# An encoder trunk in split float32 on one core: both heads' products ahead of their squares, low parts last in attention, and one transpose a tick sooner

## The chip, the cores and the metric

The kernel runs on one core of a Trainium2 chip. The metric is the device time of one execution in microseconds; a time that is quoted for a kernel is the median of several executions. One further execution is taken by the hardware profiler; all rows of a profile and a trace are from that one.

## The reference

The reference is an encoder trunk of two layers over 256 tokens of width 1024, all in float32. Cut to what the change touches, one layer is:

```python
u = rms_norm(h, g_mix_pre)
(gq, gk, gv, gg, ra_f, ra_b, aq, ak, av, gate_a, gate_b) = jnp.split(u @ w_in, offsets, axis=-1)
# branch A: gated linear attention in both directions, 4 heads, 128 keys and 256 values each
o_gla    = rms_norm(o_f + o_b, g_gla_out)            # one root per token and head
branch_a = (o_gla * silu(gg)) @ w_o_gla
# branch B: softmax attention, 8 query heads of 128, 2 key heads, all 256 tokens are keys
branch_b = gqa_attention(q, k, v) @ w_o_attn
# merge, then the output projection
mixed = sigmoid(gate_a) * branch_a + sigmoid(gate_b) * branch_b
h = h + rms_norm(mixed @ w_out, g_mix_post)
# then a SwiGLU feed-forward block and an input embedding, each added to h
```

## The kernel before, in words

**Products in three matmuls.** Each float32 operand is split into a high part, a cast to TensorE's reduced format by ScalarE (ACT), and a low part, the difference, by VectorE (DVE). Both stand in `split` (line 133). A product is then three matmuls: high by high, and each high by the other's low. `mm3` (lines 107 to 111, its matmuls carry line 105) does the three of one part one after another. `passes` (line 113, its matmuls carry line 121) takes several parts of one sum: first two matmuls of every part, then the third of every part. Without `fresh` the first two are high by high and low by high, and the last one reads the low part of the second operand. With `fresh` the low part of the first operand comes last.

**Tiles and order.** Tokens stand in two halves of 128. All PSUM tiles (`acc`, `aux`) are 128x512, one of eight banks each. Weights are streamed by DMA into `raw` or `lent` tiles, cast and subtracted into `wh` and `wl`, and used from there. Side work is written as generators that are resumed by ticks: a matmul loop over weights (`amode`) gives ticks, two for 12 matmuls of 512 columns, and `yield n` lets n ticks pass. The tables `W` and `WAIT_...` hold these numbers, and with a list of priorities they set the order in which each engine's program is written; every engine runs its own program in that order.

**GLA outputs.** `outputs(hf, pr)` (from line 1309) is called four times per layer, for each half and pair of heads. Two heads share one PSUM bank `o`, 256 columns each. For each head come six matmuls and, in the kernel before, directly behind them a Square on ACT (line 1324) that sums the squares of its 256 columns into `ss`. GpSimd (POOL) makes the inverse root (lines 465 and 466), and VectorE scales both heads out of PSUM into `on` (line 517). When all are done, `out_gate` takes the sigmoid of the output gate on ACT (line 1388), multiplies on VectorE (line 126), and PE transposes the result (line 447, tile `aux_0gg`).

**Attention.** `attend` (from line 1187) computes, for one key head and one half of the queries, the softmax, transposes the probabilities for both halves of the keys (`turn_p`, line 1176), splits them into `pT` (tiles `mid_..at`), and multiplies them with the values (`avh`, `avl`) into `aux_..at`: two parts, six matmuls of 512 columns. There are eight such products, four a layer.

**The merge.** `merge` multiplies both branches with their sigmoids; when the second is added (line 1451), a task `turn` is queued that waits `WAIT_MIX[hf]` ticks and then transposes four 128x128 blocks into `mixT` (`transpose_in`, line 447, split by line 133). The output projection (`by_half`, line 719; matmuls `acc_..wout`) reads `mixT`, half 0 first, in two parts `kh` of four blocks each. It starts with the first part of half 0.

Of the kernel before, what the change touches and what calls it, by code (L numbers as in the profile page):

```python
# [13 lines left out]
AF = mybir.ActivationFunctionType  # L14
# [3 lines left out]
P = 128  # L18
# [8 lines left out]
WAIT, WAIT_FIRST, WAIT_FFN, WAIT_BLOCK = 6, 4, 4, 6  # L27

WAIT_NEXT, WAIT_IN, WAIT_H = (7, 11), ((6, 9), (6, 6)), ((3, 5), (3, 5))
WAIT_MIX = 4, 6  # L30
WAIT_SPREAD = 12
W = dict(r=5, z=6, s0=4, s=3, s1=9, o0=1, o=1, k=4, q=3, a0=1, a1=4, a2=4, a3=1, g=6)

# [26 lines left out]
def trunk_kernel(ctx: ExitStack, tc: tile.TileContext, a: dict, out: bass.AP):  # L60
# [25 lines left out]
    def big(dt=F32):  # L86
        return bigp.tile([P, 2048], dt, tag="big", name=nm("big"))

    def mid(dt=F32):
        return b4p.tile([P, 1024], dt, tag="mid", name=nm("mid"))  # L90

    def acc():
        return accp.tile([P, 512], F32, tag="acc", name=nm("acc"))

    def aux():
        return accp.tile([P, 512], F32, tag="acc", name=nm("aux"))
# [4 lines left out]
    def small(n, tag, bufs=None):  # L101
        return smp.tile([P, n], F32, tag=tag, name=nm(tag), **({"bufs": bufs} if bufs else {}))

    def mm(o, lhsT, rhs, start, stop):
        return nc.tensor.matmul(o, lhsT, rhs, start=start, stop=stop)  # L105

    def mm3(o, l, r, start, stop):
        (lh, ll), (rh, rl) = l, r
        mm(o, lh, rh, start, False)
        mm(o, lh, rl, False, False)  # L110
        mm(o, ll, rh, False, stop)

    def passes(o, parts, start, stop, fresh=False, between=None, **kw):

        ps = [((xh, yh), (xh, yl), (xl, yh)) if fresh else ((xh, yh), (xl, yh), (xh, yl)) for (xh, xl), (yh, yl) in parts]
        seq = [p for t in ps for p in t[:2]] + [t[2] for t in ps]
        for n, (x, y) in enumerate(seq):  # L120
            nc.tensor.matmul(o, x, y, start=start and n == 0, stop=stop and n == len(seq) - 1, **kw)  # L121
            if between is not None and 2 * (n + 1) == len(seq):
                between()
# [7 lines left out]
    def split(hi, lo, src):  # L131

        return nc.scalar.copy(hi, src), nc.vector.tensor_tensor(out=lo, in0=src, in1=hi.bitcast(F32), op=ALU.subtract)  # L133
# [325 lines left out]
    def inv_sqrt(t, n, mul, add, eps=None):  # L459

        with in_turn():
            if eps is None:
                nc.gpsimd.tensor_scalar(out=t, in0=t, scalar1=mul, scalar2=add, op0=ALU.mult, op1=ALU.add)
            else:
                nc.gpsimd.tensor_scalar(out=t, in0=t, scalar1=eps, scalar2=mul, op0=ALU.add, op1=ALU.mult)
        last_pow[0] = nc.gpsimd.tensor_tensor(out=t, in0=t, in1=neghalf[:, :n], op=ALU.pow)
# [49 lines left out]
    def scale_gain(out, in0, r, g):  # L516
        nc.vector.scalar_tensor_tensor(out=out, in0=in0, scalar=r, in1=g, op0=ALU.mult, op1=ALU.mult)

    def halves(t):
        return [t[:, j * 512 : (j + 1) * 512] for j in range(2)]  # L520
# [180 lines left out]
    def project_t(sp):  # L701

        o = [acc(), acc()]
        for kh in range(2):
            wmode(o, sp, kh * 4, ws.take(), kh == 0, kh == 1)
            ws.done()
        return o

    def project(sp):

        o = [acc(), acc()]
        for kh in range(2):
            w = ws.take()
            for hf in range(2):
                amode(o[hf], sp, hf, kh * 4, w, kh == 0, kh == 1)
            ws.done()
        return o
# [81 lines left out]
    ss = [small(2, "ss") for _ in range(2)]  # L799
# [176 lines left out]
    for l in range(DEPTH):  # L976
# [108 lines left out]
        o = {}  # L1085
# [18 lines left out]
        kTh, kTl, avh, avl = (kv4[:, i * 512 : (i + 1) * 512] for i in range(4))  # L1104
# [71 lines left out]
        def turn_p(pr_):  # L1176
            res = []
            for s in range(2):
                ps = aux()
                for i in range(4):  # L1180
                    nc.tensor.transpose(ps[:, i * P : (i + 1) * P], pr_[:, i, s * P : (s + 1) * P], ident)
                pT = halves(mid(F32R))
                split(pT[0], pT[1], ps)
                res.append(pT)
            return res

        def attend(g):
            qs = []
            for hf in range(2):
                yield W["q"]  # L1190
                ps = aux()
                for i in range(4):
                    hd = 4 * g + i
                    nc.tensor.transpose(ps[:, i * P : (i + 1) * P], qrs[hf][:, hd * P : (hd + 1) * P], ident)
                qh, ql = halves(mid(F32R))
                split(qh, ql, ps)
                qs.append((qh, ql, qss[hf][:, 4 * g : 4 * g + 4]))
            keys.need()
            yield W["a0"]
            prs = []  # L1200
            for hf in range(2):
                prs.append(softmax(g, hf, qs[hf]))
                yield W["a1"]
            for hf in range(2):
                pT = turn_p(prs[hf])
                yield W["a2"]
                o = aux()
                for s in range(2):
                    vs = slice(s * 256 + g * P, s * 256 + (g + 1) * P)
                    mm3(o, (avh[:, vs], avl[:, vs]), pT[s], s == 0, s == 1)  # L1210
                aT.put(o, 4 * g, 4, hf * P, P)
                yield W["a3"]

        def attention():
            for g_ in range(2):
                part[0] = f"{l}at{g_}"
                yield from attend(g_)
# [9 lines left out]
        for x in range(2):  # L1227
            o = project_t(uT)
# [81 lines left out]
        on = big().rearrange("p (s c) -> p s c", s=2)  # L1310

        def outputs(hf, pr):

            o = aux()
            ss = small(8, "hss")
            for i in range(2):
                hd = 2 * pr + i
                c = slice(hd * 256, (hd + 1) * 256)
                oh = o[:, i * 256 : (i + 1) * 256]
                for s in range(2):  # L1320

                    idx = hf if s == hf else (2 if s == 0 else 3)
                    mm3(oh, [t[:, hd, idx, :] for t in sc], [t[:, s, c] for t in v], s == 0, s == 1)
                nc.scalar.activation(
                    on[:, hf, c], oh, AF.Square, scale=1.0 / 16.0, accum_out=ss[:, i : i + 1]
                )
            inv_sqrt(ss[:, 0:2], 2, 1.0, EPS, eps_out[hf])
            for i in range(2):
                hd = 2 * pr + i
                scale_gain(  # L1330
                    on[:, hf, hd * 256 : (hd + 1) * 256], o[:, i * 256 : (i + 1) * 256], ss[:, i : i + 1], ggla
                )
# [39 lines left out]
        for j in range(2):  # L1372
            o = project(uT)
# [72 lines left out]
        def merge(br):  # L1446
            def then(j, hf, o):
                sl = [s[:, hf, j * 512 : (j + 1) * 512] for s in sgate[: br + 1]]
                vmul(sl[br], o, sl[br])
                if br == 1:  # L1450
                    nc.vector.tensor_tensor(out=sl[0], in0=sl[0], in1=sl[1], op=ALU.add)

                    def turn():
                        yield WAIT_MIX[hf]
                        transpose_in(mixT, sl[0], 4 * j, 4, hf)
# [57 lines left out]
        for hf in range(2):  # L1513
            ws.lend = hf == 1
            for b in range(2):
                o = acc()
# [51 lines left out]
        o = []  # L1568
# [138 lines left out]
```

## Time and profile before

| | |
|---|---|
| time, median of 3 runs | 920.82 us (920.67 to 921.23) |
| profiled execution | 920.53 us, of which the span is 918.8 us |
| granted TensorE clock | 0.998 |
| TensorE (PE) busy | 909.9 us, 4673 matmuls |
| PE's weight loads (PEld) | 776.1 us |
| VectorE (DVE) | 785.2 us |
| ScalarE (ACT) | 583.1 us |
| GpSimd (POOL) | 93.1 us |
| moved by DMA | 173.44 MB, 188 GB/s over the span |

In the rows that follow, a row of the timeline has the start in us from the span's start, the busy time of the group, the engine, the line of the kernel, the operation, what it writes and reads (tile names with their numbers left out, the layer is the digit in the name), the shape, and how many instructions the row holds. Behind it, in brackets, stands the idle time ahead of it and what ended that. Ends of matmuls are modelled; their starts are not. The waits view has for each pair of waiting and releasing tile the time, how often, and the longest. The view of stretches has a stretch's length, the busy time and the number of instructions of PE in it, the granted clock, the DMA share and GB/s.

### The profile page before, as it was taken

To read this page: it belongs to the slowest core of one execution; us is meant where nothing else is said; L and a number is where in the kernel's file an instruction comes from. 1 tells how busy PE (TensorE), PEld (TensorE's weight loads), DVE (VectorE), ACT (ScalarE), POOL (GpSimd) and SP (SyncE) were. 2 spreads that over 40 slices of the span, in tenths; PEclk is the share of its full clock that TensorE was granted. 3 is DMA by queue.
4 is the path that set the end of the run, shared out by engine and by line. 5 is a ranking of instruction groups with operands and counts; after the bars stand their busy time and mean duration, and the time that the engine had idled before them with its cause. 6 is when DMAs were issued, how large, how long until landed. Compare 5 with 4: busy or idle time off the path is not lost.

```text
span 918.8 us, 12423 instructions
## 1 busy us (share of the span) xinstructions
PE 909.9 (99%) x4673; PEld 776.1 (84%) x4673; DVE 785.2 (85%) x1004; ACT 583.1 (63%) x968; POOL 93.1 (10%) x149
## 2 busy tenths in 40 slices
PE   9999999999999999999999999999999999999996
PEld 8998888888888888888899988888888888888886
DVE  6988989987669998999779789798875799989984
ACT  6688767564567565567675677765644766565563
POOL 3700212310000000000114001100001000000000
PEclk9999999999999999999999999999999999999999
DMA  8664445657385655657576424454673856555361
GB/s 277 206 199 135 138 138 189 212 184 244 107 298 183 210 197 189 244 158 260 195 238 210 158 92 138 138 202 164 201 256 103 278 170 212 215 173 225 124 243 46
DMA packets 88679, 173.44 MB, mean 189 GB/s; under 512 B 3422, under 2 KB 26470, under 8 KB 88108
## 3 DMA queue, kind: packets, MB, share of 16 engines
q1 hardware_dynamic: 88316, 172.27, 55.1%
q8 instruction: 36, 0.59, 0.3%
q10 hardware_dynamic: 304, 0.40, 0.1%
q14 instruction: 23, 0.19, 0.1%
HBM read 169.50 MB, written 3.15 MB: 188 GB/s over the span
## 4 chain that ended last, share of the span: by engine, by line
PE 92%; DVE 4%; issue 1%; ACT 1%; POOL 1%; DMA 1%; POOLq 0%; DVEq 0%; SPq 0%; ACTq 0%
PE acc_1ffnin L121 11%; PE acc_0ffnin L121 11%; PE acc_0gate L121 7%; PE acc_1gate L121 7%; PE acc_1ffnin L105 7%; PE acc_0ffnin L105 6%; PE acc_1rq L121 3%; PE acc_0gqk L121 3%; PE acc_0wout L121 2%; PE acc_1gqk L121 2%; PE acc_0ple L121 2%; PE acc_1gg L121 2%; PE acc_0v L121 2%; PE acc_0merge L121 2%; PE acc_1merge L121 2%; PE acc_1ple L121 2%
## 5 line engine op out<-in xcount | busy, mean ns | idle before, releaser
L105 PE MATMUL acc_0ffnin<-wh_0ffnin,big_0ffnin 128*128 128x512 f32 x176 | 57.0, 393 | 0.1
L105 PE MATMUL acc_1ffnin<-wh_1ffnin,big_1ffnin 128*128 128x512 f32 x176 | 56.8, 392 | 0.0
L133 ACT CAST wh_1ffnin<-raw_1ffnin 128x1024 fp32r<-128x1024 f32 x38 | 38.5, 1049 | 27.1 <-DMA raw_1ffnin<-in_w_ffn_out_dram 8.6
L133 ACT CAST wh_0ffnin<-raw_0ffnin 128x1024 fp32r<-128x1024 f32 x38 | 38.2, 1048 | 24.9 <-PE acc_0ffnin L121 7.4
L133 DVE TENSOR_TENSOR wl_1ffnin<-raw_1ffnin,wh_1ffnin 128x1024 fp32r<-128x1024 f32 x38 | 45.0, 1223 | 8.8 <-ACT wh_1ffnin L133 8.7
L133 DVE TENSOR_TENSOR wl_0ffnin<-raw_0ffnin,wh_0ffnin 128x1024 fp32r<-128x1024 f32 x38 | 44.7, 1222 | 8.1 <-ACT wh_0ffnin L133 8.0
L121 PE MATMUL acc_0ffnin<-wh_0ffnin,big_0wout 128*128 128x512 f32 x168 | 42.5, 393 | 0.0
L121 PE MATMUL acc_1ffnin<-wh_1ffnin,big_1wout 128*128 128x512 f32 x168 | 42.5, 393 | 0.0
L105 PEld LDWEIGHTS acc_0ffnin<-wh_0ffnin,big_0ffnin 128*128 128x128 f32 x176 | 33.0, 188 | 7.2 <-DVE big_0ffnin L133 0.5
L105 PEld LDWEIGHTS acc_1ffnin<-wh_1ffnin,big_1ffnin 128*128 128x128 f32 x176 | 33.0, 188 | 6.7
L133 DVE TENSOR_TENSOR wl_1ffnin<-lent_1ffnin,wh_1ffnin 128x1024 fp32r<-128x1024 f32 x30 | 35.9, 1221 | 1.7 <-ACT wh_1ffnin L133 1.7
L133 DVE TENSOR_TENSOR wl_0ffnin<-lent_0ffnin,wh_0ffnin 128x1024 fp32r<-128x1024 f32 x30 | 35.9, 1221 | 1.7 <-ACT wh_0ffnin L133 1.7
L121 PEld LDWEIGHTS acc_1ffnin<-wh_1ffnin,big_1wout 128*128 128x128 f32 x168 | 31.1, 188 | 6.2
L121 PEld LDWEIGHTS acc_0ffnin<-wh_0ffnin,big_0wout 128*128 128x128 f32 x168 | 31.1, 188 | 6.2
L133 ACT CAST wh_1ffnin<-lent_1ffnin 128x1024 fp32r<-128x1024 f32 x30 | 30.7, 1052 | 7.3 <-PE acc_1ffnin L105 3.9
L133 ACT CAST wh_0ffnin<-lent_0ffnin 128x1024 fp32r<-128x1024 f32 x30 | 30.7, 1054 | 7.0 <-PE acc_0ffnin L105 3.9
L105 PE MATMUL acc_1ffnin<-wl_1ffnin,big_1ffnin 128*128 128x512 f32 x88 | 34.3, 390 | 0.0
L105 PE MATMUL acc_0ffnin<-wl_0ffnin,big_0ffnin 128*128 128x512 f32 x88 | 34.3, 390 | 0.0
L133 DVE TENSOR_TENSOR wl_0gate<-raw_0gate,wh_0gate 128x1024 fp32r<-128x1024 f32 x20 | 24.3, 1260 | 5.3 <-ACT wh_0gate L133 5.2
L133 ACT CAST wh_0gate<-raw_0gate 128x1024 fp32r<-128x1024 f32 x20 | 20.0, 1049 | 13.1 <-DMA raw_0gate<-in_w_o_attn_dram 6.3
L133 DVE TENSOR_TENSOR wl_1gate<-raw_1gate,wh_1gate 128x1024 fp32r<-128x1024 f32 x20 | 23.6, 1223 | 5.4 <-ACT wh_1gate L133 5.2
L133 ACT CAST wh_1gate<-raw_1gate 128x1024 fp32r<-128x1024 f32 x20 | 20.0, 1049 | 11.7 <-DMA raw_1gate<-in_w_o_attn_dram 5.7
(710 smaller groups left out, 2705.4 us busy)
## 6 DMA issues: line engine op xcount, KB each, us to landing
raw_0ffnin<-in_w_ffn_out_dram SPq DMA_DIRECT2D x11, 1024.0 KB, 5.6
raw_1ffnin<-in_w_ffn_out_dram SPq DMA_DIRECT2D x11, 1024.0 KB, 5.2
lent_0ffnin<-in_w_ffn_in_dram SPq DMA_DIRECT2D x6, 1024.0 KB, 7.7
lent_1ffnin<-in_w_ffn_in_dram SPq DMA_DIRECT2D x6, 1024.0 KB, 6.7
raw_0v<-in_w_in_dram SPq DMA_DIRECT2D x4, 1024.0 KB, 4.9
raw_0gate<-in_w_o_gla_dram SPq DMA_DIRECT2D x4, 1024.0 KB, 5.2
raw_0gate<-in_w_o_attn_dram SPq DMA_DIRECT2D x4, 1024.0 KB, 5.6
raw_0wout<-in_w_ffn_in_dram SPq DMA_DIRECT2D x8, 512.0 KB, 5.0
```

The costliest lines, as they stand in the source:

```text
L105: return nc.tensor.matmul(o, lhsT, rhs, start=start, stop=stop)
L121: nc.tensor.matmul(o, x, y, start=start and n == 0, stop=stop and n == len(seq) - 1, **kw)
L133: return nc.scalar.copy(hi, src), nc.vector.tensor_tensor(out=lo, in0=src, in1=hi.bitcast(F32), op=ALU.subtract)
```

## The change

Three edits:

1. `WAIT_MIX` goes from (4, 6) to (3, 6): the transposes of a merged part of half 0 are written one tick sooner.
2. In `attend` the two calls of `mm3` become one call of `passes`: both parts' first two matmuls come first, then both that read the low part of the probabilities.
3. In `outputs` the loop is cut in two: both heads' twelve matmuls come first, then both heads' squares.

```diff
-WAIT_MIX = 4, 6
+WAIT_MIX = 3, 6
...
                 o = aux()
-                for s in range(2):
-                    vs = slice(s * 256 + g * P, s * 256 + (g + 1) * P)
-                    mm3(o, (avh[:, vs], avl[:, vs]), pT[s], s == 0, s == 1)
+                vs = [slice(s * 256 + g * P, s * 256 + (g + 1) * P) for s in range(2)]
+                passes(o, [((avh[:, c], avl[:, c]), pT[s]) for s, c in enumerate(vs)], True, True)
                 aT.put(o, 4 * g, 4, hf * P, P)
...
                     mm3(oh, [t[:, hd, idx, :] for t in sc], [t[:, s, c] for t in v], s == 0, s == 1)
+            for i in range(2):
+                c = slice((2 * pr + i) * 256, (2 * pr + i + 1) * 256)
                 nc.scalar.activation(
-                    on[:, hf, c], oh, AF.Square, scale=1.0 / 16.0, accum_out=ss[:, i : i + 1]
+                    on[:, hf, c], o[:, i * 256 : (i + 1) * 256], AF.Square, scale=1.0 / 16.0, accum_out=ss[:, i : i + 1]
                 )
```

From the second edit on, the changed kernel's lines up to the third are numbered one lower, and behind it one higher (the squares are line 1325). In the rows of each engine's program below, "waits" names the engines whose semaphores an instruction waits for, and a number at the end of a name tells tiles of one name apart.

TensorE's program in layer 0, at the third call of `outputs` (its bank is `aux_0gla_1580`; `acc_0gg` are products of the output gate's weights), as a difference:

```order
 L105 MATMUL aux_0gla_1580<-v_0v_1009,big_0gla_1171 128x256
 L105 MATMUL aux_0gla_1580<-v_0v_1008,big_0gla_1172 128x256
-L121 MATMUL acc_0gg_1448<-wh_0gg_1372,big_start_279 128x512 x2
-L121 MATMUL acc_0gg_1448<-wl_0gg_1373,big_start_279 128x512 x2
-L105 MATMUL aux_0gla_1580<-v_0v_1008,big_0gla_1171 128x256 [waits Activation_49]
+L105 MATMUL aux_0gla_1580<-v_0v_1008,big_0gla_1171 128x256
 L105 MATMUL aux_0gla_1580<-v_0v_1009,big_0gla_1171 128x256
 L105 MATMUL aux_0gla_1580<-v_0v_1008,big_0gla_1172 128x256
```

The second head's first matmul no longer waits for ACT, and the four matmuls that stood in between go behind the twelve.

TensorE's program in layer 1, at the second attention product, as a difference (`mid_1at_5093` and `mid_1at_5101` are the tiles of both key halves' probabilities, high and low part in one tile; `big_1kv` are the values):

```order
-L105 MATMUL aux_1at_5178<-mid_1at_5093,big_1kv_4573 128x512 [waits DVE_49,Activation_49]
-L105 MATMUL aux_1at_5178<-mid_1at_5093,big_1kv_4573 128x512 [waits DVE_49]
-L105 MATMUL aux_1at_5178<-mid_1at_5093,big_1kv_4573 128x512
-L105 MATMUL aux_1at_5178<-mid_1at_5101,big_1kv_4573 128x512 [waits Activation_49]
-L105 MATMUL aux_1at_5178<-mid_1at_5101,big_1kv_4573 128x512 [waits DVE_49]
-L105 MATMUL aux_1at_5178<-mid_1at_5101,big_1kv_4573 128x512
+L121 MATMUL aux_1at_5178<-mid_1at_5093,big_1kv_4573 128x512 [waits DVE_49,Activation_49]
+L121 MATMUL aux_1at_5178<-mid_1at_5093,big_1kv_4573 128x512
+L121 MATMUL aux_1at_5178<-mid_1at_5101,big_1kv_4573 128x512 [waits Activation_49]
+L121 MATMUL aux_1at_5178<-mid_1at_5101,big_1kv_4573 128x512
+L121 MATMUL aux_1at_5178<-mid_1at_5093,big_1kv_4573 128x512 [waits DVE_49]
+L121 MATMUL aux_1at_5178<-mid_1at_5101,big_1kv_4573 128x512 [waits DVE_49]
```

A wait for DVE is a wait for a low part: it moved from the second and the fifth matmul to the fifth and the sixth; the second wait for ACT, for the second high part, moved from the fourth to the third.

TensorE's program in layer 1 ahead of the output projection's second part for half 0 (`aux_1merge` are the transposes, `big_1merge` is `mixT`), first before and then after:

```order
L121 MATMUL acc_1wout_6357<-wh_1merge_6255,big_1merge_6294 128x512 x8
L121 MATMUL acc_1wout_6357<-wl_1merge_6256,big_1merge_6294 128x512 x4
L447 MATMUL aux_1merge_6382<-ident,big_1gate_5817 128x128 [waits DVE_49]
L447 MATMUL aux_1merge_6382<-ident,big_1gate_5817 128x128 x3
L447 MATMUL aux_1merge_6402<-ident,big_1gate_5817 128x128 [waits DVE_49]
L447 MATMUL aux_1merge_6402<-ident,big_1gate_5817 128x128 x3
L121 MATMUL acc_1wout_6443<-wh_1merge_6219,big_1merge_6294 128x512 [waits Activation_49]
L121 MATMUL acc_1wout_6356<-wh_1merge_6297,big_1merge_6387 128x512 [waits Activation_49]
```

```order
L121 MATMUL acc_1wout_6357<-wh_1merge_6255,big_1merge_6288 128x512 x6
L447 MATMUL aux_1merge_6376<-ident,big_1gate_5817 128x128 [waits DVE_49]
L447 MATMUL aux_1merge_6376<-ident,big_1gate_5817 128x128 x3
L121 MATMUL acc_1wout_6357<-wh_1merge_6255,big_1merge_6288 128x512 x2
L121 MATMUL acc_1wout_6357<-wl_1merge_6256,big_1merge_6288 128x512 x4
L121 MATMUL acc_1wout_6356<-wh_1merge_6297,big_1merge_6381 128x512 [waits Activation_49]
```

The four transposes of half 0's second part (6382, now 6376) stand six matmuls ahead of the product that reads them. Before, four transposes of the other half (6402) and one matmul of a later sum (6443) stood between; both go back to places further on.

ScalarE's program in layer 0 around the third and fourth calls of `outputs` (1580 and 1606), first before and then after:

```order
L133 COPY mid_0gate_1659<-mid_0gate_1652 128x512 [waits DVE_49]
L1324 ACTIVATE big_0gla_965,hss_0gla_1581<-aux_0gla_1580 128x256 [waits PE_49]
L133 COPY wh_0gg_1626<-raw_0gg_1443 128x1024 [waits DMAHW5_49,PE_49]
L133 COPY wh_0gg_1626<-raw_0gg_1443 128x1024
L1324 ACTIVATE big_0gla_965,hss_0gla_1581<-aux_0gla_1580 128x256 [waits PE_49]
L1379 ACTIVATE big_0gg_1312<-acc_0gg_1448,rs_start_121 128x512 [waits PE_49]
L1324 ACTIVATE big_0gla_965,hss_0gla_1607<-aux_0gla_1606 128x256 [waits PE_49]
L1388 ACT_TABLE_LOAD
L1388 ACTIVATE mid_0gg_1672<-big_0gg_1312 128x1024 [waits Activation_49]
L1324 ACTIVATE big_0gla_965,hss_0gla_1607<-aux_0gla_1606 128x256 [waits PE_49]
```

```order
L133 COPY mid_0gate_1659<-mid_0gate_1652 128x512 [waits DVE_49]
L1389 ACT_TABLE_LOAD
L1389 ACTIVATE mid_0gg_1672<-big_0gg_1312 128x1024 [waits Activation_49]
L1325 ACTIVATE big_0gla_965,hss_0gla_1581<-aux_0gla_1580 128x256 [waits PE_49]
L1325 ACTIVATE big_0gla_965,hss_0gla_1581<-aux_0gla_1580 128x256
L133 COPY wh_0gg_1626<-raw_0gg_1443 128x1024 [waits DMAHW5_49,PE_49]
L1325 ACTIVATE big_0gla_965,hss_0gla_1607<-aux_0gla_1606 128x256 [waits PE_49]
L1325 ACTIVATE big_0gla_965,hss_0gla_1607<-aux_0gla_1606 128x256
L133 COPY wh_0gg_1626<-raw_0gg_1443 128x1024
```

The load of the sigmoid's table and the first sigmoid stood ahead of the last square of all; now they stand ahead of the third call's two squares, and the weight casts (`wh_0gg_1626`) behind those.

## The prediction, on record before the changed kernel ran

> **What bounds the kernel now.** I read the page's first part, then the chain that ended last, then TensorE's own waits.
>
> ```profile
> PE 909.9 (99%) x4673; PEld 776.1 (84%) x4673; DVE 785.2 (85%) x1004; ACT 583.1 (63%) x968; POOL 93.1 (10%) x149
> ...
> PE 92%; DVE 4%; issue 1%; ACT 1%; POOL 1%; DMA 1%; POOLq 0%; DVEq 0%; SPq 0%; ACTq 0%
> ```
>
> ```profile
> PE aux_1at L105 <- DVE mid_1at L133: 0.2, 1, 0.2
> PE aux_0gla L105 <- ACT big_0gla L1324: 0.2, 1, 0.2
> ```
>
> TensorE (PE) is the bound: busy 99% of 918.8 us, 92% of the chain. The change takes no matmul away, so all that it can win is time in which PE stands still or restarts. The waits view names two such places that the diff touches, 0.2 us each. But matmul ends are modelled, so this view is a lower bound; I therefore measure every place by start-to-start distances against a pace taken from the same trace.
>
> The pace of a 512-column matmul: the first row below holds six, and the next row starts 1.36 us later, so **0.227 us** each. The last three rows give the transpose: 150.73 to 154.32 is 3.59 us for 16 transposes and 8 matmuls; less 8 x 0.227 that is 1.77, **0.111 us** each.
>
> ```profile
> 124.11 1.52 PE L105 MATMUL aux_0at<-mid_0at,big_0kv 128*128 128x512 f32 x6
> 125.47 0.39 PE L121 MATMUL acc_0gg<-wh_0gg,big_start 128*128 128x512 f32 x1
> ...
> 150.73 1.91 PE L447 MATMUL aux_0gg<-ident,mid_0gg 128*128 128x128 f32 x16
> 152.40 2.08 PE L121 MATMUL acc_0gate<-wh_0gg,big_start 128*128 128x512 f32 x8
> 154.32 1.07 PE L121 MATMUL acc_0gate<-wl_0gg,big_start 128*128 128x512 f32 x4
> ```
>
> **Term 1: the squares (GLA outputs).** In `outputs` the second head's six matmuls write the same PSUM bank that the first head's Square reads, and wait for it. Other matmuls were placed into the gap; the question is whether they fill it. The stretch of all four calls, from the row after the first six matmuls to the end of the last, in layer 0 and in layer 1:
>
> ```profile
> 128.41:139.58 11.17, 11.02 (x67) 1.00 0.24 90
> 587.53:598.00 10.47, 10.47 (x67) 1.00 0.26 96
> ```
>
> Same count of instructions, same clock, 0.70 us apart. The rows say where:
>
> ```profile
> 129.15 0.98 PE L105 MATMUL aux_0gla<-v_0v,big_0gla 128*128 128x256 f32 x6
> ...
> 132.10 0.98 PE L105 MATMUL aux_0gla<-v_0v,big_0gla 128*128 128x256 f32 x6
> ...
> 133.62 0.87 PE L105 MATMUL aux_0gla<-v_0v,big_0gla 128*128 128x256 f32 x6
> 134.32 0.63 PE L121 MATMUL acc_0gg<-wh_0gg,big_start 128*128 128x512 f32 x2
> 134.79 0.63 PE L121 MATMUL acc_0gg<-wl_0gg,big_start 128*128 128x512 f32 x2
> ...
> 135.33 0.19 ACT L1324 ACTIVATION_READ_ACCUMULATOR big_0gla<-aux_0gla 128x1 f32 x1
> ...
> 135.57 0.98 PE L105 MATMUL aux_0gla<-v_0v,big_0gla 128*128 128x256 f32 x6 [0.15 <-ACT big_0gla L1324]
> ...
> 138.78 0.98 PE L105 MATMUL aux_0gla<-v_0v,big_0gla 128*128 128x256 f32 x6
> ```
>
> ```profile
> 588.26 0.98 PE L105 MATMUL aux_1gla<-v_1v,big_1gla 128*128 128x256 f32 x6
> 589.08 0.86 PE L121 MATMUL acc_1gg<-wl_1gg,big_0ple 128*128 128x512 f32 x3
> ```
>
> Six undisturbed matmuls (a first head, at 133.62) show 0.87 and are followed 0.70 later. All four second heads of layer 0 show 0.98: each restarts 0.11 late, the price of one refill after a wait. At 135.57 a real gap comes on top: the two fillers of 134.79 end at 134.79 + 2 x 0.227 = 135.24, and the square's accumulator is read only at 135.33 to 135.52. That is 0.33 of standing still plus 0.11. Rows in sum: 3 x 0.11 + 0.44 = 0.77. Layer 1 has one such restart, at 588.26 (0.82 to the next row instead of 0.70): 0.12. So 10.47 - 0.12 = 10.35 is the undisturbed stretch, layer 0 loses 11.17 - 10.35 = 0.82 by the windows (I take this one, since it needs no modelled end), layer 1 loses 0.12. After the change no second head waits for a square, and the fillers do the same work behind the twelve matmuls. **Gain 0.82 + 0.12 = 0.94**; the bounds are 0.70, what the windows alone show, and 0.94, all of it.
>
> What is late next? The bank is released by L517, behind both squares and POOL's root. Squares that stand last could delay it, and with it later users of the bank; that is rival C.
>
> **Term 2: the merged half, one tick sooner.** The transposes of half 0's second part stood directly ahead of the product that reads them.
>
> ```profile
> 232.82 1.03 PE L447 MATMUL aux_0merge<-ident,big_0gate 128*128 128x128 f32 x8
> 233.61 0.98 PE L121 MATMUL acc_0wout<-wh_0merge,big_0merge 128*128 128x512 f32 x2
> 234.43 0.39 PE L121 MATMUL acc_0wout<-wl_0merge,big_0merge 128*128 128x512 f32 x1
> ```
>
> ```profile
> 690.77 1.03 PE L447 MATMUL aux_1merge<-ident,big_1gate 128*128 128x128 f32 x8
> 691.56 0.98 PE L121 MATMUL acc_1wout<-wh_1merge,big_1merge 128*128 128x512 f32 x2
> 692.38 0.39 PE L121 MATMUL acc_1wout<-wl_1merge,big_1merge 128*128 128x512 f32 x1
> ```
>
> In either layer 8 transposes and 2 matmuls take 1.61 us; by the pace 8 x 0.111 + 2 x 0.227 = 1.34. Lost 0.27, twice, although another half's transposes and one matmul already fill the wait. Now the four transposes stand six matmuls (6 x 0.227 = 1.36 us) ahead of their product. Is their source ready, and does the cast come in time?
>
> ```profile
> 685.56 0.69 DVE L1451 TENSOR_TENSOR big_1gate<-big_1gate,big_1gate 128x512 f32<-128x512 f32 x1
> ```
>
> ```profile
> 691.40 1.08 ACT L133 CAST big_1merge<-aux_1merge 128x512 fp32r<-128x512 f32 x2 [3.89 <-PE aux_1merge L447]
> ```
>
> The sum is there at 686.25, and the transposes now start near 689.9 (four 512-column matmuls before 690.77). ACT has been idle 3.89 us, begins 0.63 after the first transpose's start and needs 0.54 for one of its two casts: 689.9 + 1.17 = 691.1, while PE comes to the product at 689.9 + 4 x 0.111 + 1.36 = 691.7. Margin 0.6; in layer 0 it is larger by the embedding's four transposes, which stand between. The other half's transposes return to their own place, five microseconds before their use. **Gain 2 x 0.27 = 0.54**; bounds 0 (a cast that comes late again) and 0.54.
>
> **Term 3: low parts last in attention.** Of eight places one stands still, in layer 1:
>
> ```profile
> 543.94 0.39 PE L105 MATMUL aux_1at<-mid_1at,big_1kv 128*128 128x512 f32 x1
> 544.52 1.44 PE L105 MATMUL aux_1at<-mid_1at,big_1kv 128*128 128x512 f32 x5 [0.20 <-DVE mid_1at L133]
> 545.80 0.39 PE L121 MATMUL acc_1v<-wh_1gqk,big_0ple 128*128 128x512 f32 x1
> ```
>
> ```profile
> 543.78 1.28 DVE L133 TENSOR_TENSOR mid_1at<-aux_1at,mid_1at 128x512 fp32r<-128x512 f32 x2
> ```
>
> Six matmuls take 1.86 instead of 1.36: 0.50 lost, because the second one reads the first low part, and VectorE writes both low parts only from 543.78 to 545.06 (the first until about 544.47; PE resumes 0.05 later). Under the new order the two low parts are read by the fifth and sixth matmul. The fifth comes up at 543.94 + 4 x 0.227 = 544.85, ready. The sixth comes up at 545.07 and its part is seen at 545.06 + 0.05 = 545.11: 0.04 late, plus a refill of 0.11. So 0.15 stays and **0.35 is won**; bounds 0 (VectorE comes later still) and 0.50 (0.04 sooner). At the other seven places nothing stands still now, and low parts read later cannot wait more: 0.
>
> ```profile
> 544.52 1.00 PEld L105 LDWEIGHTS aux_1at<-mid_1at,big_1kv 128*128 128x128 f32 x5 [0.62 <-DVE mid_1at L133]
> ```
>
> Here the weight load waits together with its matmul, although the late operand is the moving one. [...]
>
> **Sum.** 0.94 + 0.54 + 0.35 = 1.83 us. The profiled execution took 920.53 (span 918.8 plus 1.7 around it), so 918.70; it lies 0.29 under the median of the three runs, 920.82, which goes to **919.0**. This is 0.2% (1.84 us, about what a measurement of this kernel can tell from no change) to within a hundredth, so "faster" and "same" split the main case about evenly.
>
> **Rivals.**
>
> A. *All stalls go.* Low parts arrive 0.04 us sooner relative to PE, or the refill isn't paid: 0.94 + 0.54 + 0.50 = 1.98, 918.8. For it: VectorE runs ahead wherever PE waited for others. Against: the row at 543.78 starts with no idle time, so VectorE is behind its own queue there. Chance 0.18.
>
> B. *Only part comes through.* The change does less than it says, because a wait returns elsewhere: only the 0.4 us that the waits view names (920.4), or the sum less one new restart of 0.3 to 1.0 us, at the merge's cast (margin 0.6) or at the output gate's transposes (919.3 to 920.0). For it: each of these margins is under 1 us. Against: ACT's 3.89 us idle time ahead of the merge's cast. Chance 0.16.
>
> C. *Slower: ACT's order in layer 0.* ACT works in its program's order, and that order changes: the sigmoid of the output gate's first half, with its table load, now stands ahead of the third call's squares, and a weight cast behind them.
>
> ```profile
> 134.53 0.62 ACT L133 CAST mid_0gate<-mid_0gate 128x512 fp32r<-128x512 f32 x1 [0.93 <-DVE mid_0gate L126]
> ...
> 138.74 1.28 ACT L1388 ACT_TABLE_LOAD   x1
> 140.03 1.06 ACT L1388 ACTIVATE mid_0gg<-big_0gg 128x1024 f32<-128x1024 f32 x1
> ```
>
> ```profile
> 138.21 1.22 DVE L133 TENSOR_TENSOR wl_0gg<-raw_0gg,wh_0gg 128x1024 fp32r<-128x1024 f32 x1
> ...
> 144.09 0.88 DVE L517 SCALAR_TENSOR_TENSOR big_0gla<-aux_0gla,hss_0gla,ggla_0gla 128x256 f32<-128x256 f32 x2 [0.59 <-POOL hss_0gla L466]
> ...
> 149.69 0.69 DVE L126 TENSOR_TENSOR mid_0gg<-mid_0gg,big_0gla 128x512 f32<-128x512 f32 x1
> ```
>
> The cast of 134.53, the load and the sigmoid then run one after another until 134.53 + 0.62 + 1.28 + 1.06 = 137.5, so the third pair of squares ends near 138.2, 0.6 later than now. The fourth call's squares gain by it: they stood behind load and sigmoid and come about 1.3 sooner. So the last scaling (144.09 now) comes about 1 us sooner; it then ends at 144.97 - 1.0. Behind it VectorE has one weight low part (1.22), one low part of attention and eight products of the gate (a pair of such a size shows 1.28 and one shows 0.69, so 0.59 apart): 1.22 + 9 x 0.59 = 6.5. That ends near 150.5, against 150.38 now. PE's sixteen transposes, at 150.73 now, come 0.82 sooner, at 149.9, and the last four of them, which need that product, at 149.9 + 12 x 0.111 = 151.2. Margin 0.7. Beyond it each microsecond of lateness costs PE one: the kernel is slower by over 0.2% if this chain comes 0.7 + 1.83 + 1.84 = 4.4 us later than worked out (922.7 and more), for instance if POOL's root, which is rough in the profile, takes two microseconds longer in two calls. In layer 1 PE's stretch loses 0.12 instead of 0.82, so its chain has less to catch up; I give it no part of this. Chance 0.06.
>
> **How the numbers follow.** The forecast, 0.60 (918.5 to 919.4, half of it under 918.98); A 0.18; B 0.16; C 0.06. Faster by over 0.2%: 0.30 + 0.18 = 0.48. Within 0.2%: 0.30 + 0.16 = 0.46. Slower: 0.06. The range reaches down to 918.4: all stalls gone, 918.8, and 0.4 for the scatter of the runs shown (0.15 below the median to 0.41 above) and of places that shift. It reaches up to 920.3, most of B: 1.83 less 1.3 of new waits.
>
> **What would show it.** Right: second heads follow first heads at once, and the stretch of the GLA outputs in layer 0 shrinks to about 10.35; 4 transposes with 6 matmuls ahead of the output projection in 1.80 us and no restart behind them; attention at its second place in layer 1 takes six matmuls in about 1.51, with a last one restarted. Wrong: a new row on PE that waits for L126 at the gate's transposes, or for the merge's cast; restarts that move onto the 256-column matmuls' followers; or an undisturbed stretch in layer 0 that is still over 11 us, which would mean that the losses were not the squares'.

## The result, and the profile after

| | before | after |
|---|---|---|
| median of 22 runs | 920.87 us (920.25 to 921.55) | 919.25 us (918.59 to 921.1) |
| ratio, with its 95% interval | | 0.9985 (0.9978 to 0.9991) |
| profiled execution, and its span | 920.53 us, 918.8 | 918.94 us, 917.2 |

The change wins 1.62 us by the medians, 0.18%: a gain clear of noise (0.8 to 2.0 us by the interval), and just inside the 0.2% that the chances were set by. The forecast was 919.0. The runs of the changed kernel scatter over 2.5 us, those of the kernel before over 1.3.

The first part of the page, the chain, and all of TensorE's waits in the changed kernel:

```profile
PE 908.5 (99%) x4673; PEld 776.5 (85%) x4673; DVE 784.2 (85%) x1004; ACT 581.8 (63%) x968; POOL 91.8 (10%) x149
...
PE 95%; ACT 1%; DVE 1%; DMA 1%; issue 1%; POOL 0%; POOLq 0%; ACTq 0%; DVEq 0%; SPq 0%
```

```profile
PE warm L105 <- POOL seed L142: 1.0, 1, 1.0
PE aux_start L142 <- DMA mid_start<-in_g_mix_pre_dram: 0.2, 1, 0.2
```

Both waits that the change was to remove, for a square and for a low part, are gone; VectorE's share of the chain fell from 4% to 1%. (The wait of `aux_start`, 0.2 us, stands in the first 5 us of the execution, where profiles of one kernel differ: the first one of the kernel before shows no such wait, its second one 0.3.)

TensorE at the GLA outputs in layer 0 after the change. The rows show twelve matmuls at once, then the fillers, without a gap:

```profile
130.33 1.60 PE L105 MATMUL aux_0gla<-v_0v,big_0gla 128*128 128x256 f32 x12
131.76 1.55 PE L121 MATMUL acc_0gg<-wh_0gg,big_start 128*128 128x512 f32 x6
133.15 1.60 PE L105 MATMUL aux_0gla<-v_0v,big_0gla 128*128 128x256 f32 x12
134.58 0.63 PE L121 MATMUL acc_0gg<-wh_0gg,big_start 128*128 128x512 f32 x2
```

The view of stretches from the first matmul of the first call to the one behind the last call, layer 0 and layer 1, in the kernel before and then in the changed kernel (length first):

```profile
127.61:139.81 12.20, 12.04 (x75) 1.00 0.27 87
586.73:598.23 11.50, 11.50 (x75) 1.00 0.30 93
```

```profile
127.41:138.78 11.37, 11.37 (x75) 1.00 0.33 97
585.51:596.87 11.36, 11.36 (x75) 1.00 0.35 97
```

The stretch holds 72 matmuls (x75 counts three that reach in from ahead). Both layers now take the same time: 0.83 us less in layer 0 and 0.14 in layer 1.

TensorE ahead of the output projection's second part in layer 1 (compare 690.77 to 692.38 before): four transposes, six matmuls, and then the part that reads the transposed half, 0.23 apart from its first row on, so nothing restarts:

```profile
688.02 0.60 PE L447 MATMUL aux_1merge<-ident,big_1gate 128*128 128x128 f32 x4
688.38 0.71 PE L121 MATMUL acc_1wout<-wh_1merge,big_1merge 128*128 128x512 f32 x2
688.93 1.09 PE L121 MATMUL acc_1wout<-wl_1merge,big_1merge 128*128 128x512 f32 x4
689.85 0.39 PE L121 MATMUL acc_1wout<-wh_1merge,big_1merge 128*128 128x512 f32 x1
690.08 0.39 PE L121 MATMUL acc_1wout<-wl_1merge,big_1merge 128*128 128x512 f32 x1
```

TensorE at attention's second place in layer 1 (before: 543.94 to 545.80), and VectorE's low parts there:

```profile
543.00 1.69 PE L121 MATMUL aux_1at<-mid_1at,big_1kv 128*128 128x512 f32 x6
544.53 1.80 PE L121 MATMUL acc_1v<-wh_1gqk,big_0ple 128*128 128x512 f32 x7
```

```profile
542.85 1.28 DVE L133 TENSOR_TENSOR mid_1at<-aux_1at,mid_1at 128x512 fp32r<-128x512 f32 x2
```

Six matmuls take 1.53 us, where 1.86 were needed before and 1.36 is the pace.

**Where the time went, point by point.** The table compares the starts of the same TensorE instruction in both traces; the lead is how much earlier the changed kernel is there.

| place | before | after | lead |
|---|---|---|---|
| GLA outputs, layer 0, begin | 127.62 | 127.42 | 0.20 |
| behind them | 139.82 | 138.79 | 1.03 |
| seam: transposes ahead of layer 1 | 472.36 | 471.05 | 1.31 |
| seam: some 4 us later | 476.60 | 475.67 | 0.93 |
| attention, layer 1, begin | 543.94 | 543.00 | 0.94 |
| behind it | 545.80 | 544.53 | 1.27 |
| GLA outputs, layer 1, begin | 586.74 | 585.52 | 1.22 |
| behind them | 598.24 | 596.88 | 1.36 |
| output projection, layer 1, behind | 705.74 | 704.11 | 1.63 |
| transposes of the second half's pre-norm | 717.96 | 716.12 | 1.84 |
| last group of matmuls | 911.14 | 909.35 | 1.79 |
| span | 918.8 | 917.2 | 1.6 |

The steps that were forecast add up to 0.83 (GLA outputs, layer 0) + 0.28 (to the seam, the merge in it) + 0.33 (attention) + 0.14 (GLA outputs, layer 1) + 0.27 (to behind the output projection) = 1.85. Two steps were not forecast: at the start of layer 1, which I call the seam, 0.38 is lost again, and behind the output projection of layer 1 another 0.21 is won.

### The profile page after: what moved, and what is told of

It is laid out like the page before. It is cut to its first block, busy times and chain, and to the rows that moved or that the text cites. A ratio compares the mean times of both kernels' runs of the same rounds, so it can differ in the third digit from the quotient of the medians.

```text
span 917.2 us, 12424 instructions
## 1 busy us (share of the span) xinstructions
PE 908.5 (99%) x4673; PEld 776.5 (85%) x4673; DVE 784.2 (85%) x1004; ACT 581.8 (63%) x968; POOL 91.8 (10%) x149
## 4 chain that ended last, share of the span: by engine, by line
PE 95%; ACT 1%; DVE 1%; DMA 1%; issue 1%; POOL 0%; POOLq 0%; ACTq 0%; DVEq 0%; SPq 0%
PE acc_1ffnin L121 12%; PE acc_0ffnin L121 12%; PE acc_0gate L121 7%; PE acc_1gate L121 7%; PE acc_0ffnin L105 7%; PE acc_1ffnin L105 7%; PE acc_1gqk L121 3%; PE acc_0gqk L121 3%; PE acc_0wout L121 2%; PE acc_1wout L121 2%; PE acc_1v L121 2%; PE acc_0gg L121 2%; PE acc_1gg L121 2%; PE acc_0v L121 2%; PE acc_1merge L121 2%; PE acc_0merge L121 2%
```

## The experiments

Theory: TensorE loses the time only at the places that the prediction named, each place by itself, and the squares' part of it because the second head shares a bank with a square that is being read. Rivals: that the order on ScalarE and VectorE and not the bank makes the difference; that only the 0.4 us of the waits view can be won; and, once the trace was there, that a transfer at the seam gives back a part. Each kernel below was timed beside the kernel before on the same chip, 11 runs of each experiment (12 in one); the two repeats without an edit are one profiled execution each. The ratio with its interval is worked out over all runs, so it can differ a little from the quotient of the two medians.

**The squares alone.** Edit: only the third part of the change.

> Only the squares are moved behind both heads. Theory (second heads wait for a square in their bank, nothing else): the stretch of the GLA outputs shrinks to about 10.35 us in both layers, 0.86 us in layer 0 and 0.16 in layer 1 by the trace of the changed kernel, so up to 1.0 us faster, 919.9 from 920.87; no stall returns elsewhere. Rival (the waits view is right and only its 0.2 us per kind can be won): 0.2 us, 920.7. Rival (what layer 0 wins is partly given back where layer 1 starts, since the first weights of layer 1 land by the stream's time and not by TensorE's): 0.6 to 0.8 us, about 920.2, with a new wait near 475 us.

Measured: 920.1 us against 920.88, ratio 0.9987 (0.9979 to 0.9996). In its trace the stretch of 72 matmuls at the GLA outputs takes 11.36 us in both layers, 0.84 and 0.14 less than before; the wait for low parts in attention is still there with 0.2. TensorE loses 0.09 at the seam. The gain of 0.8 by the medians (0.4 to 1.9 by the interval) is more than the 0.2 of the waits view, which falls as a rival: three restarts of 0.11 each are no wait to that view.

**The tick alone.** Edit: `WAIT_MIX = 3, 6` and nothing else.

> Only the wait of the merged half goes from 4 to 3 ticks. Theory: 0.25 us in layer 0 and 0.24 in layer 1, 0.5 in all, 920.4; in the trace the eight transposes and the restart ahead of the output projection's second part become four transposes without a restart. Rival (the cast's chain only moves and the product waits for it as before): 0, 920.9.

Measured: 920.89 us against 920.88, ratio 0.9998 (0.9989 to 1.0007). By the time alone this would be the rival's 0. The trace says otherwise: 0.25 us are won at the merge of layer 0, 0.24 at that of layer 1, and 0.21 behind it, but 0.51 go at the seam in this execution. The interval holds 0.5 us too, so the time can't decide; the rows do.

**The low parts alone.** Edit: `passes` in `attend` and nothing else.

> Only the low parts of the probabilities are multiplied last. Theory: seven of the eight places give nothing, the second in layer 1 gives 0.32 to 0.35 us (six matmuls in 1.53 instead of 1.86), so 920.5. Rival (the low parts come so late that the sixth matmul waits as long as the second did): 0 to 0.1, 920.8. Rival (everything at that place goes): 0.50, 920.4.

Measured: 920.46 us against 920.88, ratio 0.9993 (0.9984 to 1.0002). TensorE at the place in this kernel:

```profile
543.99 1.68 PE L121 MATMUL aux_1at<-mid_1at,big_1kv 128*128 128x512 f32 x6
545.51 0.85 PE L121 MATMUL acc_1v<-wh_1gqk,big_0ple 128*128 128x512 f32 x3
```

Six matmuls in 1.52, as the theory said, 0.33 won; the other places change by 0.01 at most. At the seam this execution loses 0.59.

**A bank for each head.** The squares stay behind each head, but no head shares its bank.

```diff
-            o = aux()
+            o = [aux(), aux()]
...
-                oh = o[:, i * 256 : (i + 1) * 256]
+                oh = o[i][:, 0:256]
```

> The kernel before with each head's products in a PSUM bank of its own, so the second head has no square to wait for although the squares stand behind each head as before; four calls now take eight banks. Theory (the wait is for the bank that the square reads): the second heads follow without a gap, and the stretches shrink as with the squares moved, 0.86 and 0.16 us, unless a call waits for a bank that the scaling still holds; a stall of that kind would be on VectorE's scaling and costs some tenths in each call. Rival (the gain comes from the order on ScalarE and VectorE, not from the bank): stretches as long as before, 11.2 in layer 0, and no gain.

Measured: 921.14 us against 920.88, ratio 0.9998 (0.9989 to 1.0007), so no gain. But the two stretches of 72 matmuls take 11.36 us here as well: with banks of their own the second heads don't wait, although the squares stand behind each head. In this kernel, too, the twelve matmuls of a call stand directly one behind another, with the fillers behind them. But fillers between the heads cost nothing by themselves: in layer 1 of the kernel before, the last call's second head stands behind five fillers and comes up after the first head's square has ended (596.91 + 0.23 = 597.14), and it takes the undisturbed 0.72:

```profile
596.91 0.23 ACT L1324 ACTIVATION_READ_ACCUMULATOR big_1gla<-aux_1gla 128x1 f32 x1
597.29 0.89 PE L105 MATMUL aux_1gla<-v_1v,big_1gla 128*128 128x256 f32 x6
598.01 0.40 PE L121 MATMUL acc_1gate<-wh_1gg,big_0ple 128*128 128x512 f32 x1
```

So the wait for the shared bank is the cause. What was won in layer 0, 0.86, is given back 23 us further on, at the branch gates:

```profile
161.88 0.63 PE L121 MATMUL acc_0gate<-wl_0gate,big_start 128*128 128x512 f32 x2
162.91 0.74 PE L121 MATMUL acc_0gate<-wl_0gate,big_start 128*128 128x512 f32 x2 [0.40 <-DVE wl_0gate L133]
```

Between these rows two matmuls should take 0.45 us and take 1.03: VectorE is late with a weight's low part. By its rows the order of its program changed: two products (L129) that stood ahead of the last scaling, at 136.87 and 137.60, come behind it, at 143.28 and 144.00, and from there to the late low part VectorE is never idle. Another 0.44 us goes ahead of 270 us, at the start of layer 0's feed-forward block, where ScalarE waits 2.36 us for a piece of weights instead of 1.66. So rival C's kind of thing, a chain behind the GLA outputs that comes late, does exist in this kernel; the change as it was made stays clear of it.

**Layer 0 alone, layer 1 alone.** Edits: all three parts under `if l == 0` in one kernel and `if l == 1` in the other.

> All three edits in layer 0 alone. Stalls that go: 0.86 us at the GLA outputs, 0.25 at the merge, nothing in attention, so TensorE is 1.11 us sooner at the end of layer 0. Theory of the seam: at the start of layer 1 ScalarE stands idle until a 1 MB piece of the first weights has landed; by the traces so far every microsecond of that idle time above 0.74 delays TensorE near 475 us by one (idle 0.65: 0; 0.84: 0.10; 1.11: 0.39; 1.25: 0.51; 1.33: 0.59). So 0.0 to 0.6 is given back there, and the gain is 0.5 to 1.1 us, 919.8 to 920.4. Rival (no seam, each stall counts in full): 1.11, 919.8 in every execution.

> All three edits in layer 1 alone, behind the seam. Stalls that go: 0.16 us at the GLA outputs, 0.33 in attention, 0.24 at the merge, 0.73 in all. If the seam varied only because layer 0 was changed, it costs nothing here and the kernel is 0.73 us faster, 920.15, with ScalarE's idle time at the seam as before (0.65). If the landing varies by itself, the idle time is anywhere from 0.6 to 1.4 and the gain scatters between 0.1 and 0.73.

Measured: layer 0 alone 920.02 us against 920.69, ratio 0.999 (0.9981 to 0.9999); layer 1 alone 919.89, ratio 0.9992 (0.9984 to 1.0001). The places win what they won in the changed kernel (0.86 and 0.25 in layer 0; 0.34, 0.16, 0.24 and again 0.23 behind the output projection in layer 1). ScalarE at the seam, first in the kernel before, then in the changed one, then with layer 1 alone, whose program up to this point is that of the kernel before:

```profile
466.22 2.06 ACT L133 CAST wh_0ple<-raw_0ple 128x1056 fp32r<-128x1056 f32 x2 [0.65 <-DMA raw_0ple<-in_w_in_dram]
```

```profile
465.37 2.06 ACT L133 CAST wh_0ple<-raw_0ple 128x1056 fp32r<-128x1056 f32 x2 [1.11 <-DMA raw_0ple<-in_w_in_dram]
```

```profile
466.84 2.05 ACT L133 CAST wh_0ple<-raw_0ple 128x1056 fp32r<-128x1056 f32 x2 [1.51 <-DMA raw_0ple<-in_w_in_dram]
```

In brackets stands how long ScalarE waited for the transfer. With layer 1 alone it waits 1.51 us and TensorE loses 0.78 at the seam, though nothing had been edited ahead of it. So the edits of layer 0 aren't what makes the transfer late.

**The piece in two transfers.** The changed kernel, and the late piece of the weights loaded by halves.

```diff
-        plan += [unit_rows(w, n, C_RA, C_RA + 1056, FIRST if l + n == 0 else None) for n in range(4)]
+        plan += [unit_rows(w, n, C_RA, C_RA + 1056, FIRST if (l, n) in ((0, 0), (1, 2)) else None) for n in range(4)]
```

> The changed kernel, with the late piece of the first weights of layer 1 loaded by two transfers of half its size, so that its first cast waits for the first half alone. TensorE's program is the same. Theory of the seam: the piece's second cast ends about 1 us sooner, the new wait near 475 us goes, 0.39 us in the profile against the changed kernel and less scatter: 918.6 to 918.9 against its 919.25. Rival (the wait at the seam has another cause, for instance VectorE's order): no difference, 919.25. Rival (two smaller transfers land later than one): slower, 919.5.

Measured: 919.88 us against 920.69, ratio 0.9991 (0.9982 to 1.0). ScalarE's casts of the two halves, and what TensorE waits for longest:

```profile
465.50 1.08 ACT L133 CAST wh_0ple<-raw_0ple 128x1056 fp32r<-128x1056 f32 x1 [1.52 <-DMA raw_0ple<-in_w_in_dram]
...
467.36 1.07 ACT L133 CAST wh_0ple<-raw_0ple 128x1056 fp32r<-128x1056 f32 x1
```

```profile
PE aux_0ple L447 <- DVE mid_0ple L517: 1.2, 1, 1.2
```

The remedy did not work, and the reason is not that of the last rival, though ScalarE waits no less for the first half (1.52). The issue of the transfer on SyncE's queue (here of the first half), and a square on ScalarE that belongs to the norms ahead of the transposes, in this kernel and then in the kernel before:

```profile
460.46 0.34 SPq L297 DMA_DIRECT2D raw_0ple<-in_w_in_dram  x1
...
466.48 0.41 ACT L497 ACTIVATE mid_0ple<-mid_0ple 128x256 f32<-128x256 f32 x1
```

```profile
460.68 0.37 SPq L297 DMA_DIRECT2D raw_0ple<-in_w_in_dram  x1
...
465.05 0.43 ACT L497 ACTIVATE mid_0ple<-mid_0ple 128x256 f32<-128x256 f32 x1
```

The first half took 5.04 us from its issue to its cast (460.46 to 465.50); the whole piece took 5.39 to 6.40 in the other twelve profiles. So, counted from its issue, it landed sooner. But ScalarE came to it sooner still, because its order changed: the cast of the first half now stands ahead of two copies (L966) and of that square (L497), all of which stood ahead of the cast of the whole. The square comes at 466.48 instead of 465.05. By the rows, the chain behind it (POOL's root, the new `h`, a second norm, VectorE's scaling L517) comes later with it, and TensorE waits 1.2 us for that scaling and loses 1.34 at the seam. The second half's cast waits for no transfer. This is one execution, moreover the slowest of its 12 runs (923.5 us against a median of 919.88); by the times this kernel isn't told from the changed one.

**Both kernels once more.** The kernel before and the changed kernel, without any edit, in a further profile each.

> The kernel before, unchanged, profiled once more, to see what varies from one execution to the next without any edit. If the landing at the seam varies by itself, ScalarE's idle time ahead of the late piece differs from 0.65 us by some tenths, and TensorE's time lost near 472 to 476 us with it, while the stalls at the GLA outputs, in attention and at the merge stay within 0.03 us. If it is set by the program, the seam shows 0.65 and no loss again.

> The changed kernel, unchanged, profiled once more. Theory: the stretches at the GLA outputs, in attention and at the merge take the same time as in its first profile within 0.03 us (the edits win 1.84 there), while ScalarE's idle time at the seam and the 0.39 us lost behind it differ from 1.11 us, since they hang on when one transfer lands. If the seam's idle time is set by the program, it is 1.11 and 0.39 again.

Measured: 920.65 and 918.97 us. ScalarE at the seam, kernel before and then changed kernel:

```profile
466.11 2.05 ACT L133 CAST wh_0ple<-raw_0ple 128x1056 fp32r<-128x1056 f32 x2 [0.60 <-DMA raw_0ple<-in_w_in_dram]
```

```profile
465.56 2.06 ACT L133 CAST wh_0ple<-raw_0ple 128x1056 fp32r<-128x1056 f32 x2 [1.50 <-DMA raw_0ple<-in_w_in_dram]
```

The named places repeat to 0.02 us in both (GLA stretches 12.20 and 11.50, against 11.36 and 11.37; attention 1.85 against 1.51). The seam doesn't: the changed kernel shows 1.50 now and loses 0.76, where it showed 1.11 and lost 0.39. So the seam differs from one execution to the next without any edit. Over the twelve profiles with that transfer whole, ScalarE's wait there and what TensorE then lost against the first profile of the kernel before run along one line: 0.50, 0.60 and 0.65: nothing; 0.84: 0.09 and 0.10; 1.05: 0.29; 1.11: 0.39; 1.25: 0.51; 1.33: 0.59; 1.50: 0.76 and 0.78; 1.51: 0.78. Above about 0.73 each microsecond costs one. In all twelve ScalarE is ready for the cast 4.89 us after the issue of the transfer; what differs is how long the piece takes, 5.39 to 6.40 us from its issue to the cast.

**Another tick.** The changed kernel with `WAIT_MIX = 2, 6`.

> The changed kernel with the merged half turned one more tick sooner (2 in place of 3), some ten matmuls ahead of its use instead of six. Theory: at 3 ticks the cast is already there in time (no restart of TensorE ahead of the second part of the output projection), so a further tick wins nothing: 919.25 as the changed kernel, and the two places take the same time. It costs nothing either as long as the sum that is turned is ready: it is done about 2 us ahead. Rival (one tick still leaves a hidden wait): 0.2 to 0.5 faster. Rival (the transposes now wait for the sum or hold back weight casts on VectorE): 0.2 to 0.5 slower, with a wait for VectorE on them.

Measured: 919.06 us against 920.91, ratio 0.9986 (0.9977 to 0.9995), as the changed kernel's 0.9985. The merges win 0.25 and 0.24 us against the kernel before, as with 3 ticks. Six matmuls of distance were enough.

**Low parts first on VectorE.** The changed kernel with precedence for the probabilities' parts.

```diff
+                with tc.high_priority(AHEAD):
-                split(pT[0], pT[1], ps)
+                    split(pT[0], pT[1], ps)
```

> The changed kernel with both parts of the transposed probabilities given precedence on ScalarE and VectorE. Theory: the 0.11 us that is left at attention's second place in layer 1 (a sixth matmul that restarts) comes from VectorE, which makes the low part behind two products of the decays; with precedence it goes, 0.11 us. What is pushed back are the decays' products, for which the GLA scores in layer 0 wait: a new wait there of 0.2 to 1 us would turn this into a loss, 919.3 to 920.1. Rival (nothing else waits for them): 919.15.

Measured: 918.55 us against 920.91, ratio 0.998 (0.9971 to 0.9989). TensorE at the place:

```profile
542.44 1.52 PE L121 MATMUL aux_1at<-mid_1at,big_1kv 128*128 128x512 f32 x6
543.80 1.52 PE L121 MATMUL acc_1v<-wh_1gqk,big_0ple 128*128 128x512 f32 x6
```

Six matmuls in 1.36, the pace: the whole 0.50 of the place is won, and nothing new waits in layer 0 (its lead behind the GLA outputs grows by the same 0.86). This kernel has the lowest median of all, and its gain over the kernel before is clear of noise. Against the changed kernel the intervals overlap, and the edit's place accounts for only 0.17 of the 0.7 us between the medians. The profile shows no more than that: this execution loses nothing at the seam, but 0.8 near 872 to 875 us, and its span is 917.3, where the changed kernel's is 917.2. There ScalarE waits longer for another piece of weights, first in the changed kernel, then in this one:

```profile
863.81 2.00 ACT L133 CAST wh_1ffnin<-raw_1ffnin 128x1024 fp32r<-128x1024 f32 x2 [4.70 <-DMA raw_1ffnin<-in_w_ffn_out_dram]
```

```profile
864.19 2.00 ACT L133 CAST wh_1ffnin<-raw_1ffnin 128x1024 fp32r<-128x1024 f32 x2 [5.95 <-DMA raw_1ffnin<-in_w_ffn_out_dram]
```

By these rows the seam is not the only place where a transfer that takes longer costs TensorE time. The profiled execution of the kernel with two halves shows the same wait with 6.16.

## Why the prediction was right

**What bounds the kernel, and the method.** Measuring by start-to-start distance against the trace's own pace was right, and the waits view alone would have given 0.4.

**Term 1, 0.94.** Measured 0.97: 0.83 and 0.14 by the stretches. The undisturbed stretch was forecast at 10.35; 11.36 less the first six matmuls (0.79) and the last filler (0.24), which that stretch left out, is 10.33. The two banks show that the shared bank is what was waited for.

**What was late next.** The margin at the output gate's transposes was forecast as 0.7 us and is more. VectorE's fourth scaling and its last products, and TensorE's transposes there, in the changed kernel:

```profile
141.96 0.87 DVE L517 SCALAR_TENSOR_TENSOR big_0gla<-aux_0gla,hss_0gla,ggla_0gla 128x256 f32<-128x256 f32 x2
...
148.09 1.29 DVE L126 TENSOR_TENSOR mid_0gg<-mid_0gg,big_0gla 128x512 f32<-128x512 f32 x2
```

```profile
149.68 1.91 PE L447 MATMUL aux_0gg<-ident,mid_0gg 128*128 128x128 f32 x16
```

The products end at 149.38, forecast 150.5, and the last four transposes, twelve times 0.111 behind 149.68, come at 151.0: 1.6 us of margin. The fourth scaling came at 141.96, 2.1 sooner than before, where I gave it 1.0: its squares end 1.6 sooner (139.88, before 141.45), and POOL's two instructions behind them take 1.0 us instead of 2.5, as far as spans on POOL can be trusted. Rival C was thus further off than I had it.

**Term 2, 0.54.** Measured 0.49 at the two merges, as one tick is enough and a second wins nothing. But the term was too small by a step that I had in front of me. Ahead of half 0's second part stood, as the filler of the wait, one matmul of half 1's sum. The change sends it back, so half 0's sum is done one matmul (0.227) sooner, and the chain of norms that starts from it runs sooner. In layer 1 TensorE waits for that chain near 717 us. ScalarE ahead of a copy in it, in the kernel before and the changed one:

```profile
709.68 0.59 ACT L451 COPY mid_1wout<-aux_1wout 128x512 f32<-128x512 f32 x1 [2.09 <-DVE big_1wout L133]
```

```profile
707.83 0.59 ACT L451 COPY mid_1wout<-aux_1wout 128x512 f32<-128x512 f32 x1 [1.87 <-DVE big_1wout L133]
```

It waits 0.22 less for VectorE. All seven profiles with the tick in layer 1 show 0.21 to 0.26 won there, those without it at most 0.04. That the displaced matmul is the way to it is read from rows and not tried by itself.

**Term 3, 0.35.** Measured 0.33, with the restart of the sixth matmul that was forecast: six matmuls take 1.51 to 1.53 in every profile with the edit in layer 1, against 1.51 forecast; only with precedence on VectorE does the restart go (1.36). The load of the sixth matmul in the changed kernel:

```profile
544.18 0.19 PEld L121 LDWEIGHTS aux_1at<-mid_1at,big_1kv 128*128 128x128 f32 x1 [0.31 <-DVE mid_1at L133]
```

It stood idle 0.31 and started with its matmul, which waited for VectorE; the next matmul came 0.34 later instead of 0.227. In the same six, the first load stands 0.22 ahead of its matmul (542.78 and 543.00). So the refill that rival A left open was paid here. The 0.11 at the squares looks the same: in the kernel before, the load of a second head starts with its matmul (129.15), behind a wait for the square, and that of an undisturbed first head 0.23 ahead of its matmul (133.62):

```profile
129.14 0.78 PEld L105 LDWEIGHTS aux_0gla<-v_0v,big_0gla 128*128 128x128 f32 x6 [0.30 <-ACT big_0gla L1324]
...
133.39 0.89 PEld L105 LDWEIGHTS aux_0gla<-v_0v,big_0gla 128*128 128x128 f32 x6
```

**The sum.** 1.83 was forecast. The named places give 0.97 + 0.49 + 0.33 = 1.79, and with the chain behind the merge 2.0. The profile shows 1.59, since 0.38 was lost at the seam; the first microseconds gave a lead of 0.20, and behind the last matmuls 0.19 of the lead was lost (1.79 there, 1.6 in the span). The medians show 1.62. Rival B named the right size (a new wait of 0.3 to 1.0 us) at the wrong places: the wait stands where layer 1 begins, it hangs on a transfer, and it comes and goes from one execution to the next. The changed kernel doesn't run into it by being earlier: its transfer is issued 1.31 sooner too (459.37, before 460.68), which is TensorE's lead there. Why the piece takes longer in some executions, and how often, a few profiles of each kernel can't say; that stays open. Nor is a wider scatter a mark of the changed kernel: in the three later series the runs of the kernel before scatter over 2.2, 2.8 and 2.0 us.

That the places came out at 1.79 of 1.83 is the forecast's own merit. That the whole came out so near is in part luck: in this profile the 0.21 that term 2 left out makes up for half of the 0.38 that the seam took, and in the other profiles with the piece whole the seam takes from nothing to 0.78.

## What to carry to other kernels

A TensorE that is 99% busy still restarts: compare start-to-start distances with the trace's own pace, layer against layer, and add up losses such as the 0.11 us here, which no waits view names. Where a later writer of a PSUM bank waits for an earlier reader, try all writers ahead of the first reader, or banks of their own (here either order took the stretch in layer 0 from 12.20 us to 11.37 or 11.36), and see whether the reader's chain has a margin behind it (with banks of their own the 0.86 was lost again, at a weight's late low part). Where a wait is filled with later work, look what that work displaces: here the filler had cost a chain 0.22 us further on; and where the gains are this small, profile each kernel twice before a difference of 0.4 us is put down to an edit. Where a remedy fails, see first whether it changed an engine's order, as the two halves did here.

## What was not expected of the hardware

One 1 MB piece of weights took different times in executions of programs that are equal up to it: 5.54 and 5.49 us from its issue to its cast in the kernel before, 6.40 in the kernel with layer 1 alone, whose program is the same until there. Over twelve profiles it took 5.39 to 6.40. A half of it, issued at the same place, took 5.04 in the one profile that has it.
